# One wide matmul for a high weight and both parts of the input, in three of seven products of a fast matrix multiplication

## The chip, the cores and the metric

The kernel runs on one core of a Trainium2 chip. The metric is the device time of one execution in microseconds, the median of several runs. The engines are PE (TensorE, the matmuls), DVE (VectorE), ACT (ScalarE), POOL (GpSimd) and SP (SyncE, which here only issues DMAs).

## The reference

One layer of a decoder with two token mixers side by side; width 2048, 512 tokens, batch 1, all in float32. Cut to what matters:

```python
mod = silu(c) @ w_ada + b_ada
shift, scale, gate = split(mod, 3)
h = rmsnorm(x, attn_norm_g) * (1 + scale) + shift
proj = h @ w_in
q_lat, kv_lat, k_rope, z_mla, u, v, z_sgu, g_mla, g_sgu = split_cols(proj, IN_SPLITS)
...
y_mla = causal_mla_attention(q_nope, q_rope, k_nope, k_rope, v_mla) * silu(z_mla)
y_sgu = chunked_causal_sgu(u, v, sgu_norm_g, w_spatial, b_spatial) * silu(z_sgu)
merged = sigmoid(g_mla) * y_mla + sigmoid(g_sgu) * y_sgu
x = x + gate * (merged @ w_out)
return rmsnorm(x, final_norm_g)
```

`w_in` has 2048 rows; the five column blocks z_mla, g_mla, u, z_sgu and g_sgu are 2048 columns each. The attention has 16 heads with a rotary part of 64 columns whose key (`k_rope`) all heads share; its query and value come from the normalised latents `q_lat` (768) and `kv_lat` (512).

## The kernel before

**Arithmetic.** A float32 operand is split into a high part that PE takes at full speed and a low part, high plus low being the value. ACT copies the high part, DVE subtracts it from the value for the low part. A product is three matmuls into one PSUM bank: wH·xH, wH·xL and wL·xH (`mm3`, lines 135 to 137). Weights are split as they arrive, the input's parts `hh` and `hl` lie in 16 chunk tiles of 128 channels x 512 tokens each.

**Stages.** Up to 348 us: modulation, latents, v, and one plain tile of columns. From 348.2 to 1136.5 us: most column tiles (of 128 columns) of those five blocks, in 38 pairs (`PAIRS`, lines 34 to 36). Then attention, head by head, and the output projection.

**The slots.** A pair is a 2x2 block matrix product (two column tiles by two halves of the channels, against two halves of the channels by two halves of the tokens), done with seven products of sums of blocks instead of eight. A product is one slot: 8 chunks x 3 matmuls of 128x256 (lines 1267 to 1269). There are 266 slots, in an order written by hand, for a pair in the middle:

```python
turn_ = [(1, k), (6, k), (3, k - 1), (7, k), (4, k - 1), (5, k), (2, k)]
```

Products 1 to 4 of a pair write one bank ("y"), 6 and 7 another ("z"), 5 a third ("w"); `bank_for` gives the bank, always its first 256 columns. After its slot, a product is evacuated (`evacuate`): 1, 6, 2 and 4 are copied by ACT, 5, 3 and 7 are added or subtracted by DVE. When both halves of a column tile are there, `finish` puts the gate's operations (sigmoid on ACT, products on DVE) some slots later (`gate_op`). The right operand of product 4 and 5 is a token half of chunks 8 to 15 (`hh[8 + c][:, toks]` and the same of `hl`), that of product 7 the sum tiles `s4h` and `s4l`.

**What sets the order.** The program is written slot by slot; in each slot the events run in phases: evacuation of the slot ahead, FIRST, EVAC, GATE, SPLIT (the weights of the slot after next: ACT's copy, DVE's subtraction), BACK, then the slot's matmuls, then MISC and LOAD. BACK holds work for other stages (rotary tables, the spatial gating unit, the latents' norms), placed by a planner: `place` puts a job of so many us of DVE into the first slot whose charged time stays within 2.75 us; `spend` charges what is fixed. A tile is written again only when its readers are done, and so is a bank.

**Jobs named below.** `rope` computes the rotary tables on DVE in the first slots. Late in the stretch, `lat_store` writes the normalised latents to memory, `rope_load` fetches the tables (line 1122: eight DMAs on SP), `key_load` fetches the shared rotary key (line 1132: two DMAs), `key_turn` turns it on PE four slots later (line 1138), `key_rotary` rotates it on DVE in three jobs. The planner's slots for these are: tables computed up to slot 20, last latent norm 218, `key_load` 237, `key_turn` 241, key rotated by slot 245. The last pair's weights come in quarters (line 633). After the last slot, PE goes on with the rotary part of the query (`rproj`, 18 matmuls of 512 columns into bank 0), the query projection (`qproj`) of head 0 and its key projection (`kproj`).

Of the kernel before, what the change touches and what calls it, by code (L numbers as in the profile page):

```python
# [11 lines left out]
F32 = mybir.dt.float32  # L12
# [8 lines left out]
P = 128  # L21
# [94 lines left out]
def trunk_layer(ctx, tc, xT, xn, c, vecs, pos, wada, w1, w2, wv, wv3, wv4, wh, wh15, wq, wqr, wk, wvv, wo, wsT, bsp, gfin, out,  # L116
# [218 lines left out]

    hh, hl = [None] * KC, [None] * KC
    ssx = cosT
# [33 lines left out]
    for j in range(KC):  # L371
# [32 lines left out]
    def fix_to(n, between=None):  # L404
# [277 lines left out]
    for s in range(n_slots):  # L682
        def both(s=s):
            split_low(*split(s))
        on(s - 2, SPLIT, both)
    for k, pair in enumerate(PAIRS):
        at_ = slot_of[k]
        spend(at_[6] - 2, 1.22)
        for p, f in by_transfer(k).items():
            if not f:  # L690
                spend(at_[p] - 2, 1.22)
        for p in range(1, 8):
            spend(at_[p] - 2, 1.22)
# [58 lines left out]
    def evacuate(p, k, s):  # L752

        ps = bank_for(p, k)
        if p == 1:
# [7 lines left out]
        elif p == 5:  # L763
            t = res[k, "a"][:, left]
            tt(t, ps, t, ALU.add)
        elif p == 3:
            t = res[k, "b"][:, right]
            tt(t, t, ps, ALU.subtract)
        elif p == 4:
            ACT.copy(res[k, "a"][:, right], ps)  # L770
        if (p == 7 and slot_of[k][2] < slot_of[k][7]) or (p == 2 and slot_of[k][7] < slot_of[k][2]):
            def c12():
                t = res[k, "b"][:, left]
                tt(t, bank_for(7, k), t, ALU.subtract)
            if p == 7:
# [415 lines left out]

    def quarter(chunks, toks):
        return lambda c: (hh[chunks * 8 + c][:, toks], hl[chunks * 8 + c][:, toks])

    rights = {1: quarter(0, left), 2: sums_of("s2"), 3: quarter(0, right), 4: quarter(1, right), 5: quarter(1, left),
              6: sums_of("s1"), 7: sums_of("s4")}

# [58 lines left out]
    for s, (p, k) in enumerate(order):  # L1256
# [6 lines left out]
        for c in range(8):  # L1263
            xh, xl = rt_(c)
# [15 lines left out]

    place = {}
    for n, tag in (("krh", "hh10"), ("krl", "hl10"), ("m1", "hh11"), ("m2", "hl11"), ("r", "hh12"), ("qsa", "hl12"),
                   ("qsb", "hh13"), ("pt1", "hl13"), ("th0", "hh14"), ("tl0", "hl14"), ("th1", "hh15"), ("tl1", "hl15")):
        place[n] = (hp.p, tag)
# [377 lines left out]
```

## Time and profile before

| | |
|---|---|
| median of 3 runs | 1609.59 us (1609.11 to 1610.01) |
| profiled execution | 1609.98 us, its span 1608.3 us |
| PE busy | 1594.2 us, 99% of the span, 10760 matmuls |
| DVE busy | 1165.3 us, 72% |
| ACT busy | 755.5 us, 47% |
| POOL busy | 105.4 us, 7% |
| mean granted clock of PE | 0.999 |
| DMA | 329.64 MB, 205 GB/s over the span |

The span is the profiled execution between its first and last instruction. PE's busy time counts pipelined matmuls without their overlap, so a matmul's cost is read from the distance of starts, not from its duration.

### The profile page before, as it was taken

What the parts mean: (1) busy time and instruction counts of PE and PEld (TensorE: products, weight loads), DVE (VectorE), ACT (ScalarE), POOL (GpSimd) and SP (SyncE); (2) the same over time, 40 slices, a digit from 0 to 9 for tenths busy, and PEclk for the clock granted to TensorE, in tenths of its full rate; (3) what the DMA queues carried; (4) which work ended last, traced back from release to release, by engine and by line L of the source; (5) the groups of instructions that cost most, each with busy time, mean ns of one, the idle gap of its engine ahead of it and who ended that gap; (6) DMA issues with size and microseconds to landing.
All of it is one profiled execution on the core that took longest, in us unless ns stands there. A gap on an engine that the chain in (4) does not pass through costs nothing.

```text
span 1608.3 us, 26988 instructions
## 1 busy us (share of the span) xinstructions
PE 1594.2 (99%) x10760; PEld 1488.5 (93%) x10760; DVE 1165.3 (72%) x1719; ACT 755.5 (47%) x1259; POOL 105.4 (7%) x128
## 2 busy tenths in 40 slices
PE   9999999999999999999999999999999999999997
PEld 8888889999999999999999999999988889888886
DVE  8989679658777777777677777666777888763453
ACT  4443334355545454454465554554655554542322
POOL 0000000001111111111111111112000000000000
PEclk9999999999999999999999999999999999999999
DMA  9988489568899897898887998887422233336422
GB/s 379 354 296 317 171 280 324 170 193 202 219 253 252 226 252 214 233 258 212 231 253 203 250 268 207 238 193 181 162 87 88 82 105 89 90 109 227 136 87 105
DMA packets 122766, 329.64 MB, mean 205 GB/s; under 512 B 14072, under 2 KB 35600, under 8 KB 115856
## 3 DMA queue, kind: packets, MB, share of 16 engines
q1 hardware_dynamic: 104768, 269.72, 48.0%
q0 software_dynamic: 17872, 58.20, 20.8%
q8 instruction: 84, 1.38, 0.3%
q14 instruction: 42, 0.34, 0.1%
HBM read 303.95 MB, written 23.93 MB: 204 GB/s over the span
## 4 chain that ended last, share of the span: by engine, by line
PE 90%; DVE 4%; DMA 2%; ACT 1%; issue 1%; SPq 0%; DVEq 0%; ACTq 0%
PE ps L1267 15%; PE ps L1269 15%; PE ps L1268 15%; PE ps L136 14%; PE ps L137 14%; PE ps L135 14%; PE ps L1429 1%; DVE wada L126 1%; PE ps L1392 1%; PE ps L1393 1%; DVE t L123 1%; DMA wraw<-in_w 1%; DMA lat<-v_d 1%; DVE lat L123 1%; DMA rope_d<-half 0%
## 5 line engine op out<-in xcount | busy, mean ns | idle before, releaser
L106 DVE TENSOR_TENSOR w0l<-wraw,w0h 128x1024 fp32r<-128x1024 f32 (+3 forms) x74 | 78.8, 1066 | 58.8 <-ACT w0h L105 58.5
L105 ACT CAST w1h<-wraw 128x1024 fp32r<-128x1024 f32 (+3 forms) x74 | 63.9, 863 | 118.8 <-PE ps L137 57.7
L1267 PE MATMUL ps<-hh,w0h 128*128 128x256 f32 x416 | 118.5, 285 | 0.9 <-DVE lat L123 0.9
L105 ACT CAST w0h<-wraw 128x1024 fp32r<-128x1024 f32 (+3 forms) x74 | 68.9, 931 | 106.6 <-PE ps L137 66.5
L1269 PE MATMUL ps<-hh,w0l 128*128 128x256 f32 x416 | 117.7, 283 | 0.0
L1268 PE MATMUL ps<-hl,w0h 128*128 128x256 f32 x416 | 117.7, 283 | 0.0
L106 DVE TENSOR_TENSOR w1l<-wraw,w1h 128x1024 fp32r<-128x1024 f32 (+3 forms) x74 | 73.1, 988 | 59.6 <-ACT w1h L105 58.6
L1267 PE MATMUL ps<-hh,w2h 128*128 128x256 f32 x400 | 113.5, 284 | 0.0
L1267 PE MATMUL ps<-hh,w1h 128*128 128x256 f32 x400 | 113.4, 283 | 0.0
L1268 PE MATMUL ps<-hl,w1h 128*128 128x256 f32 x400 | 113.2, 283 | 0.0
L1269 PE MATMUL ps<-hh,w2l 128*128 128x256 f32 x400 | 113.2, 283 | 0.0
L1268 PE MATMUL ps<-hl,w2h 128*128 128x256 f32 x400 | 113.2, 283 | 0.0
L1269 PE MATMUL ps<-hh,w1l 128*128 128x256 f32 x400 | 113.2, 283 | 0.0
L126 DVE SCALAR_TENSOR_TENSOR wada<-wada,cact 128x2048 f32<-128x2048 f32 x47 | 107.1, 2280 | 0.0
L123 DVE TENSOR_TENSOR w2l<-raw,w2h 128x1024 fp32r<-128x1024 f32 x56 | 68.5, 1224 | 39.0 <-ACT w2h L649 38.9
L136 PE MATMUL ps<-w0l,hh 128*128 128x256 f32 (+3 forms) x288 | 92.7, 322 | 0.1
L135 PE MATMUL ps<-w0h,hh 128*128 128x256 f32 (+3 forms) x288 | 92.7, 322 | 0.0
L137 PE MATMUL ps<-w0h,hl 128*128 128x256 f32 (+3 forms) x288 | 92.4, 321 | 0.0
L135 PE MATMUL ps<-hh,w1h 128*128 128x512 f32 x226 | 89.7, 397 | 0.0
L136 PE MATMUL ps<-hl,w1h 128*128 128x512 f32 x226 | 88.3, 391 | 0.8 <-DVE hl L126 0.8
L137 PE MATMUL ps<-hh,w1l 128*128 128x512 f32 x226 | 88.1, 390 | 0.0
L629 POOL DMA_DIRECT2D wraw<-in_wh x67 | 59.2, 939 | 439.8 <-DVE w0l L123 211.7
(350 smaller groups left out, 5400.5 us busy)
## 6 DMA issues: line engine op xcount, KB each, us to landing
raw<-in_wh SPq DMA_DIRECT2D x105, 512.0 KB, 6.9
wada<-in_wada SPq DMA_DIRECT2D x47, 1024.0 KB, 7.4
wraw<-in_wh POOLq DMA_DIRECT2D x67, 512.0 KB, 6.9
wraw<-in_wh SPq DMA_DIRECT2D x45, 512.0 KB, 7.8
raw<-in_wh POOLq DMA_DIRECT2D x42, 512.0 KB, 7.8
wraw<-in_wo SPq DMA_DIRECT2D x32, 512.0 KB, 3.7
half<-in_w SPq DMA_DIRECT2D x35, 256.0 KB, 5.4
wraw<-in_w SPq DMA_DIRECT2D x16, 512.0 KB, 8.9
```

Source lines behind the costliest of these rows:

```text
L105: self.nc.scalar.copy(hi[:, :n], raw[:, :n])
L106: self.nc.vector.tensor_tensor(out=lo[:, :n], in0=raw[:, :n], in1=hi[:, :n].bitcast(F32), op=ALU.subtract)
L123: DVE.tensor_tensor(out=out, in0=in0, in1=in1, op=op)
L126: DVE.scalar_tensor_tensor(out=out, in0=in0, scalar=scalar, in1=in1, op0=op0, op1=op1, **kw)
L135: PE.matmul(ps, ah, bh, start=start, stop=False)
L136: PE.matmul(ps, ah, bl, start=False, stop=False)
L137: PE.matmul(ps, al, bh, start=False, stop=stop)
L629: q_.dma_start(t, wh[h, n, q // 10 - 1], **eng)
L1267: PE.matmul(ps, wH[:, sl], xh, start=st, stop=False, skip_group_check=True)
L1268: PE.matmul(ps, wH[:, sl], xl, start=False, stop=False, skip_group_check=True)
L1269: PE.matmul(ps, wL[:, sl], xh, start=False, stop=sp, skip_group_check=True)
L1392: PE.matmul(ps, q2[:, q], krh[:, :n], start=False, stop=False)
```

## The change

For products 4, 5 and 7 (`WIDE`), wH·xH and wH·xL become one matmul: the moving operand is `[xH | xL]` with 2 x 256 columns, and the bank's two halves take one product each; wL·xH is added into the first half as before. A slot of these has 16 matmuls instead of 24. The two halves are put together at the evacuation by one more DVE add of 128x256 per product. For this, `hh` and `hl` of a chunk become one tile of two parts (`parts_tiles`), and so do `s4h` and `s4l`. The evacuation of product 5 moves four slots later (one slot for the last pair). The planner charges each job 0.07 us less, and its limit becomes 2.7 us, 2.6 in a wide slot. The scratch tiles of attention are placed in the new tiles.

```diff
+WIDE = (4, 5, 7)
...
+    def parts_tiles(j):
+
+        hx[j] = nt(hp.p, [P, 2, S], F32R, f"h{j}")
+        return hx[j][:, 0], hx[j][:, 1]
...
+                sums["s4"] = nt(c1[0].p, [P, 8, 2, 256], F32R, "s4")
+                sums["s4h"], sums["s4l"] = sums["s4"][:, :, 0], sums["s4"][:, :, 1]
...
     def spend(s, us):
-        busy[s] = busy.get(s, 0.0) + us
+        busy[s] = busy.get(s, 0.0) + max(us - 0.07, 0.0)
 
     def place(s, us, f, *a):
 
-        while busy.get(s, 0.0) + us > 2.75:
+        while busy.get(s, 0.0) + us - 0.07 > (2.6 if 0 <= s < n_slots and order[s][0] in WIDE else 2.7):
             s += 1
...
+    def w_slot(k):
+
+        return slot_of[k][5] + (4 if k < n_pairs - 1 else 1)
...
-        for s in (at_[5] + 1, at_[3] + 1, at_[7] + 1 if at_[7] > at_[2] else at_[2] + 2):
-            spend(s, 0.42)
+        for p, s in ((5, w_slot(k)), (3, at_[3] + 1), (7, at_[7] + 1 if at_[7] > at_[2] else at_[2] + 2)):
+            spend(s, 0.84 if p in WIDE else 0.42)
+        spend(at_[4] + 1, 0.42)
...
+    def low_half(p, k):
+
+        return bank_for(p, k)[:, 256:]
...
         elif p == 5:
-            t = res[k, "a"][:, left]
-            tt(t, ps, t, ALU.add)
+            def c11():
+                t = res[k, "a"][:, left]
+                tt(t, ps, t, ALU.add)
+                tt(t, low_half(5, k), t, ALU.add)
+            on(w_slot(k), EVAC, c11)
...
         elif p == 4:
-            ACT.copy(res[k, "a"][:, right], ps)
+            t = res[k, "a"][:, right]
+            ACT.copy(t, ps)
+            tt(t, low_half(4, k), t, ALU.add)
...
-                tt(t, bank_for(7, k), t, ALU.subtract)
+                tt(t, bank_for(7, k)[:, :256], t, ALU.subtract)
+                tt(t, low_half(7, k), t, ALU.add)
...
+    rights = {1: quarter(left), 2: sums_of("s2"), 3: quarter(right), 4: lambda c: hx[c + 8][:, :, right],
+              5: lambda c: hx[c + 8][:, :, left], 6: sums_of("s1"), 7: lambda c: sums["s4"][:, c]}
...
-            PE.matmul(ps, wH[:, sl], xh, start=st, stop=False, skip_group_check=True)
-            PE.matmul(ps, wH[:, sl], xl, start=False, stop=False, skip_group_check=True)
-            PE.matmul(ps, wL[:, sl], xh, start=False, stop=sp, skip_group_check=True)
+            if p in WIDE:
+                x = rt_(c)
+                PE.matmul(ps.rearrange("p (e w) -> p e w", e=2), wH[:, sl], x, start=st, stop=False, skip_group_check=True)
+                xh = x[:, 0]
+            else:
+                xh, xl = rt_(c)
+                PE.matmul(ps[:, :256], wH[:, sl], xh, start=st, stop=False, skip_group_check=True)
+                PE.matmul(ps[:, :256], wH[:, sl], xl, start=False, stop=False, skip_group_check=True)
+            PE.matmul(ps[:, :256], wL[:, sl], xh, start=False, stop=sp, skip_group_check=True)
```

The planner's slots become: rotary tables computed up to slot 16, last latent norm 253, `key_load` 254, `key_turn` 258, key rotated by slot 265.

DVE in slot 6 (first the split made in slot 5, `w2l`, last that of slot 6; `lat<-ps` is an evacuation of product 7, `rx` and `half` are rotary work). Before:

```order
L123 TENSOR_TENSOR w2l_3324<-raw_301_3014,w2h_3323 128x1024
L123 TENSOR_TENSOR lat_350_3328<-lat_321_3131,lat_349_3327 128x512
L987 CAST rx_3135<-half_325_3137 128x128
L130 TENSOR_SCALAR rx_3135<-rx_3135,vec_88 128x128
L132 TENSOR_SCALAR rx_3135<-rx_3135 128x128
L123 TENSOR_TENSOR lat_335_3217<-ps_334_3192,lat_335_3217 128x256
L123 TENSOR_TENSOR w1l_3369<-raw_338_3248,w1h_3368 128x1024
```

Now:

```order
L124 TENSOR_TENSOR w2l_3277<-raw_268_2981,w2h_3276 128x1024
L124 TENSOR_TENSOR lat_317_3281<-lat_288_3102,lat_316_3280 128x512
L124 TENSOR_TENSOR rx_3106<-rx_3106 128x128
L133 TENSOR_SCALAR rx_3106<-rx_3106 128x128
L124 TENSOR_TENSOR rx_3106<-rx_3106 128x128
L131 TENSOR_SCALAR rx_3106<-rx_3106 128x128 x2
L133 TENSOR_SCALAR half_291_3107<-rx_3106 128x128
L124 TENSOR_TENSOR lat_302_3184<-ps_301_3159,lat_302_3184 128x256 x2
L124 TENSOR_TENSOR w1l_3326<-raw_305_3207,w1h_3325 128x1024
```

Product 7 has a second add, and six rotary operations stand here in the place of three.

SP's queue around the key's loads (`half<-kr_d`; `wraw` and `raw` are weights, `latn_d` is a store of the latents, `rope_d` the rotary tables). Before:

```order
L629 DMA wraw_1390_11618<-in_wh 128x1024
L748 DMA g_d_132<-lat_1351_11302 128x512
L629 DMA wraw_1394_11655<-in_wh 128x1024
L1132 DMA half_1399_11691<-kr_d 128x4x64 x2
L748 DMA g_d_132<-lat_1360_11375 128x512
L629 DMA raw_1403_11725<-in_wh 128x1024
L629 DMA raw_1408_11784<-in_wh 128x1024
L629 DMA raw_1416_11855<-in_wh 128x1024
```

Now:

```order
L638 DMA wraw_1407_11323<-in_wh 128x2x128 x4
L638 DMA raw_1412_11362<-in_wh 128x2x128 x4
L1091 DMA latn_d_130<-half_1390_11176 128x512
L1142 DMA cosT_11421<-rope_d 32x4x128 x4
L1142 DMA sinT_11422<-rope_d 32x4x128 x4
L1152 DMA half_1423_11453<-kr_d 128x4x64 x2
L634 DMA raw_1430_11512<-in_wh 128x1024
```

The key's loads stood between loads of weights; now they stand behind the last pair's quarter loads, the last store of the latents and the eight table loads.

DVE at the end of the slots (`w1l` and `w0l` with `wraw` are the splits for the rotary and the query projection, `hl` or `h` the low parts of the latents, `lat<-ps` the evacuations, `rx` the key's last rotary sum). Before:

```order
L106 TENSOR_TENSOR w1l_12606<-wraw_74_12522,w1h_12605 128x768
L126 SCALAR_TENSOR_TENSOR hl_1507_12610<-b_1485_12479,vec_88,hh_1506_12609 128x512
L126 SCALAR_TENSOR_TENSOR hl_1509_12614<-b_1486_12481,vec_88,hh_1508_12613 128x512
L126 SCALAR_TENSOR_TENSOR hl_1511_12618<-b_1487_12483,vec_88,hh_1510_12617 128x512
L123 TENSOR_TENSOR lat_1471_12369<-ps_1512_12621,lat_1471_12369 128x256
L126 SCALAR_TENSOR_TENSOR hl_1515_12652<-b_1488_12485,vec_88,hh_1514_12651 128x512
L126 SCALAR_TENSOR_TENSOR hl_1517_12656<-b_1489_12487,vec_88,hh_1516_12655 128x512
L106 TENSOR_TENSOR w0l_12684<-wraw_75_12555,w0h_12683 128x768
L123 TENSOR_TENSOR lat_1479_12435<-lat_1479_12435,lat_1513_12649 128x512
```

Now:

```order
L107 TENSOR_TENSOR w1l_11785<-wraw_74_11709,w1h_11784 128x768
L127 SCALAR_TENSOR_TENSOR h_1470_11788<-b_1450_11667,vec_88,h_1470_11788 128x512
L127 SCALAR_TENSOR_TENSOR h_1471_11791<-b_1451_11669,vec_88,h_1471_11791 128x512
L127 SCALAR_TENSOR_TENSOR h_1472_11794<-b_1452_11671,vec_88,h_1472_11794 128x512
L124 TENSOR_TENSOR lat_1434_11547<-ps_1473_11797,lat_1434_11547 128x256 x2
L124 TENSOR_TENSOR rx_11585<-lat_1459_11686,lat_1460_11687 128x512
L127 SCALAR_TENSOR_TENSOR h_1475_11821<-b_1453_11673,vec_88,h_1475_11821 128x512
L127 SCALAR_TENSOR_TENSOR h_1476_11824<-b_1454_11675,vec_88,h_1476_11824 128x512
L107 TENSOR_TENSOR w0l_11844<-wraw_75_11744,w0h_11843 128x768
L124 TENSOR_TENSOR lat_1434_11547<-ps_1433_11522,lat_1434_11547 128x256
```

The two products of the last pair that end here have second adds, the key's rotary sum has come in, and the last add, for product 4, stands behind the split for the query projection.

## Rows read from the trace of the kernel before

**Rows 1.** The page, part 1: busy us (share of the span) x instructions.
```profile
PE 1594.2 (99%) x10760; PEld 1488.5 (93%) x10760; DVE 1165.3 (72%) x1719; ACT 755.5 (47%) x1259; POOL 105.4 (7%) x128
```

**Rows 2.** Busy times by window: the stretch of the 266 slots.
```profile
core 0: us, PE busy (x) PEld busy (x) DVE busy (x) ACT busy (x) POOL busy (x), PEclk, DMA share, GB/s
...
348.20:1136.50 788.30, 785.63 (x6536) 783.63 (x6535) 577.17 (x751) 409.05 (x610) 101.84 (x117) 1.00 0.86 226
```

**Rows 3.** Timeline of PE in the slots (start us, us, instruction).
```profile
802.36 0.28 PE L1267 MATMUL ps<-s1h,w0h 128*128 128x256 f32 x1
...
805.24 0.28 PE L1267 MATMUL ps<-hh,w2h 128*128 128x256 f32 x1
```

**Rows 4.** Timeline of PE, late in attention.
```profile
1441.97 0.39 PE L135 MATMUL ps<-w0h,b 128*128 128x512 f32 x1
...
1445.37 0.39 PE L135 MATMUL ps<-w0h,b 128*128 128x512 f32 x1
```

**Rows 5.** Groups of DVE by form, 340 to 1140 us (busy, mean ns).
```profile
L123 DVE TENSOR_TENSOR lat<-lat,lat 128x512 f32<-128x512 f32 x91 | 62.3, 684 | 0.6
...
L123 DVE TENSOR_TENSOR lat<-ps,lat 128x256 f32<-128x256 f32 x76 | 31.8, 419 | 13.5 <-PE ps L1269 13.5
```

**Rows 6.** Timeline of DVE in the rotary work of before.
```profile
371.39 0.28 DVE L123 TENSOR_TENSOR rx<-rx 128x128 f32<-128x128 f32 x1
...
372.58 1.22 DVE L123 TENSOR_TENSOR w0l<-raw,w0h 128x1024 fp32r<-128x1024 f32 x1
373.71 0.22 DVE L132 TENSOR_SCALAR half<-rx 128x128 f32<-128x128 f32 x1
373.96 0.29 DVE L123 TENSOR_TENSOR half<-rx,half 128x128 f32<-128x128 f32 x1
```

**Rows 7.** Timeline of SP: rotary tables; last pair's loads.
```profile
993.04 2.21 SPq L1122 DMA_DIRECT2D cosT<-rope_d  x4
995.30 5.36 SPq L1122 DMA_DIRECT2D sinT<-rope_d  x4
1000.75 0.38 SPq L629 DMA_DIRECT2D raw<-in_wh  x1
...
1093.09 2.58 SPq L633 DMA_DIRECT2D wraw<-in_wh  x4
1095.78 2.62 SPq L633 DMA_DIRECT2D raw<-in_wh  x4
```

**Rows 8.** The rotary key's tensor in memory: its DMAs.
```profile
L1132 SPq DMA_DIRECT2D half<-kr_d x2: 695/748/800, 1052.0 to 1052.8; - x2
...
DMA to landing us min/median/max: 1.7/3.6/10.3
```

**Rows 9.** Timeline of PE: slot 218, the key's turn, the hand-over.
```profile
994.90 0.28 PE L1267 MATMUL ps<-s4h,w1h 128*128 128x256 f32 x1
...
1065.85 0.60 PE L1138 MATMUL ps<-ident,half 128*128 128x128 f32 x4
...
1136.48 0.40 PE L135 MATMUL ps<-hh,w1h 128*128 128x512 f32 x1
...
1144.66 0.39 PE L135 MATMUL ps<-hh,w1h 128*128 128x512 f32 x1
```

**Rows 10.** Timeline of DVE up to the hand-over.
```profile
1127.03 1.23 DVE L123 TENSOR_TENSOR w0l<-raw,w0h 128x1024 fp32r<-128x1024 f32 x1 [3.60 <-ACT w0h L649]
...
1139.13 0.95 DVE L106 TENSOR_TENSOR w0l<-wraw,w0h 128x768 fp32r<-128x768 f32 x1
```

**Rows 11.** Timeline of ACT at the hand-over.
```profile
1137.98 0.63 ACT L730 ACTIVATE lat<-lat 128x512 f32<-128x512 f32 x1 [0.93 <-DVE lat L123]
...
1143.16 0.62 ACT L105 CAST w1h<-wraw 128x512 fp32r<-128x512 f32 x1
```

**Rows 12.** Waits of DVE, 348 to 1165 us (total, times, longest).
```profile
DVE w2l L123 <- ACT w2h L649: 65.2, 63, 5.4
...
DVE w0l L123 <- ACT w0h L649: 59.5, 62, 3.6
```

More of the change, by code (lines that the diff above doesn't have):

```diff
@@ L334, in trunk_layer @@
         load_before(gv[0] + st + 1 if st < 31 else gv[0] + 31, ada_load, 2 * KC + j)
-    hh, hl = [None] * KC, [None] * KC
+    hh, hl, hx = [None] * KC, [None] * KC, [None] * KC
+    def parts_tiles(j):
+        hx[j] = nt(hp.p, [P, 2, S], F32R, f"h{j}")
+        return hx[j][:, 0], hx[j][:, 1]
     ssx = cosT
@@ L376, in trunk_layer @@
         wH, wL = get(g1[j], ahead=0)
-        hh[j] = nt(hp.p, [P, S], F32R, f"hh{j}")
-        hl[j] = nt(hp.p, [P, S], F32R, f"hl{j}")
+        hh[j], hl[j] = parts_tiles(j)
         ACT.activation(hh[j], xt[j], AF.Copy, scale=A)
@@ L421, in fix_to @@
         for j, t in zip(js, ts_):
-            hh[j] = nt(hp.p, [P, S], F32R, f"hh{j}")
+            hh[j], hl[j] = parts_tiles(j)
             ACT.activation(hh[j], t, AF.Identity, bias=shift[:, j:j + 1])
@@ L426, in fix_to @@
         for j, t in zip(js, ts_):
-            hl[j] = nt(hp.p, [P, S], F32R, f"hl{j}")
             stt(hl[j], t, shift[:, j:j + 1], hh[j].bitcast(F32), ALU.add, ALU.subtract)
@@ L693, in trunk_layer @@
             spend(at_[p] - 2, 1.22)
-        for s in (at_[5] + 1, at_[3] + 1, at_[7] + 1 if at_[7] > at_[2] else at_[2] + 2):
-            spend(s, 0.42)
-        for s, (ty, _) in ((max(at_[4], at_[5]), pair[0]), (max(at_[3], at_[7]), pair[1])):
+        for p, s in ((5, w_slot(k)), (3, at_[3] + 1), (7, at_[7] + 1 if at_[7] > at_[2] else at_[2] + 2)):
+            spend(s, 0.84 if p in WIDE else 0.42)
+        spend(at_[4] + 1, 0.42)
+        for s, (ty, _) in ((max(at_[4], w_slot(k) - 1), pair[0]), (max(at_[3], at_[7]), pair[1])):
             spend(s + 3, 1.38 if ty == "s" else 0.69)
@@ L715, in bank_for @@
     def bank_for(p, k):
-        return open_bank[k, "y" if p in (1, 2, 3, 4) else "z" if p in (6, 7) else "w"][:, :256]
+        return open_bank[k, "y" if p in (1, 2, 3, 4) else "z" if p in (6, 7) else "w"]
+    def low_half(p, k):
+        return bank_for(p, k)[:, 256:]
     gs, bs = {}, {}
@@ L752, in evacuate @@
     def evacuate(p, k, s):
-        ps = bank_for(p, k)
+        ps = bank_for(p, k)[:, :256]
         if p == 1:
@@ L781, in evacuate @@
         if p == max((4, 5), key=lambda q: slot_of[k][q]):
-            finish(k, "a", s + 1)
+            finish(k, "a", max(s, w_slot(k)) + 1)
     for j in range(8):
@@ L1182, in lat_split @@
     def lat_split(i):
-        lh[i] = nt(hp.p, [P, S], F32R, f"hh{i}")
-        ll[i] = nt(hp.p, [P, S], F32R, f"hl{i}")
+        lh[i], ll[i] = parts_tiles(i)
         g = vec[:, C_GQ + i:C_GQ + i + 1]
@@ L1190, in sums_of, with quarter @@
         return lambda c: (sums[name + "h"][:, c], sums[name + "l"][:, c])
[L1192 to L1196, printed above, removed]
+    def quarter(toks):
+        return lambda c: (hh[c][:, toks], hl[c][:, toks])
+    rights = {1: quarter(left), 2: sums_of("s2"), 3: quarter(right), 4: lambda c: hx[c + 8][:, :, right],
+              5: lambda c: hx[c + 8][:, :, left], 6: sums_of("s1"), 7: lambda c: sums["s4"][:, c]}
     def to_attention():
@@ L1279, in trunk_layer @@
         lat_split(i)
[L1281 to L1284, printed above, removed]
+    place, kept = {}, {}
+    for n, *where in (("krh", 10, 0), ("krl", 10, 1), ("m1", 11, 0), ("m2", 11, 1), ("r", 12, 0), ("pt1", 12, 1),
+                      ("qsa", 13, 0), ("qsb", 13, 1), ("th0", 14, 0), ("tl0", 14, 1), ("th1", 15, 0), ("tl1", 15, 1)):
+        place[n] = where
     for n, tag in zip(("vh0", "vl0", "qh", "ql", "kh", "kl", "vh1", "vl1", "pt3", "pt2", "th2"), range(11)):
-        place[n] = (latp.p, f"lat{tag}")
-    place["tl2"] = (latp.p, "rx")
+        place[n] = f"lat{tag}"
+    place["tl2"] = "rx"
     def at(name, dt, shape=(P, S)):
-        p, tag = place[name]
-        return nt(p, list(shape), dt, tag)
+        if isinstance(place[name], str):
+            return nt(latp.p, list(shape), dt, place[name])
+        i, e = place[name]
+        if i not in kept:
+            kept[i] = parts_tiles(i)
+        t = kept[i][e]
+        return t if dt is F32R else t.bitcast(F32)
     krh, krl = at("krh", F32R), at("krl", F32R)
```

3 lines of the change are left out of this document (removed).

## The prediction

> **What bounds the kernel now.** The page comes first: PE is busy for 1594.2 of 1608.3 us [rows 1], so an end that moves must move with PE's queue: fewer or shorter matmuls, or another wait in it. Next, the change touches only the 266 slots of the column pairs, so I read that stretch alone: from 348.2 to 1136.5, PE is busy for 785.63 of 788.30 us with a granted clock of 1.00, the 2.4 GHz level, which leaves 2.7 us of waiting in the whole stretch; DVE is busy for 577.17 us, 73% [rows 2]. So in this stretch the slots cost what the matmul stream costs. Then the stream itself: 24 matmuls of 256 columns start between 802.36 and 805.24 [rows 3], which is 120.0 ns each and 2.88 us for a slot. DVE has room on average, but it has to deliver three things on time: the low parts of the weights for the slot after next, the sum out of a bank before PE writes that bank again, and planned work for later stages. Where it runs late, PE waits.
>
> The sum is made on the profiled execution, 1609.98 us (1608.3 of span and 1.7 around it); the median of the runs shown, 1609.59, is 0.39 lower, so the result is carried over as a difference to the median.
>
> **Term 1, the matmuls.** In the slots of products 4, 5 and 7, eight pairs of 256-column matmuls become eight of 512 columns: 38 x 3 x 8 = 912 instructions fewer. The nearest rows for a 512-column matmul on this engine at the same clock are in attention's end: 15 start between 1441.97 and 1445.37 [rows 4], 226.7 ns each. Two of 256 columns take 240.0, so each merge saves 13.3 ns, a wide slot takes 8 x (226.7 + 120.0) = 2.77 us instead of 2.88, and 912 x 13.3 ns = **12.2 us** is the gross gain. It lies wholly on the path, since PE is the bound. The rows show that two starts cost more than one, by 13.3 ns for the same columns; I take that. The other end is 0: the operand of products 4 and 5 now consists of two pieces of 256 columns that don't lie side by side, and no row of before has a matmul with such an operand.
>
> The Trainium skill ("TensorE: Matmul & The Clock Gate", section "Back-to-back issue gap") gives for a lone matmul at the high clock a spacing of the columns over 2.4 plus 2.5 ns, which speaks against the change. By it, a merge would save only the 2.5 ns, an estimate of 2.3 us in all, and with the losses below the kernel would end at 1616.4. The rows above show 13.3 in the place of its 2.5.
>
> **Term 2, the adds on DVE.** Each wide product needs one more add of 256 columns out of the bank: 114 of them. Such an add takes 419 ns [rows 5], and as consecutive operations start some 0.08 us before the modelled end of the one ahead (a split of 1.22 us at 372.58, the next at 373.71 [rows 6]), I count 0.34, or 0.46 where it needs the result of the add just ahead of it. Together 39 to 52 us on DVE, which makes 616 to 629 of some 776 us, 80%. As a total this hides under PE and costs nothing. If that cover goes locally, PE waits; there are three places where it does.
>
> *The rotary work at the start (slots 6 to 8).* From one split to the next in slot 6, DVE now has the gate's product of 512 columns (684 ns [rows 5], so 0.60), six rotary operations, both adds of product 7 (0.80) and the split itself (1.13). Five rotary operations stand between 371.39 and 372.58 and one between 373.71 and 373.96 [rows 6]: 1.44. That makes 3.97 us against a slot of 2.77 to 2.88, 1.1 to 1.2 behind; in the order of before, the same slot holds three rotary operations and one add (0.60 + 0.72 + 0.34 + 1.13 = 2.79). The next slot has four rotary operations, 0.96, + 0.80 + 1.13 = 2.9 and stays behind. Queued behind this is the subtraction of product 3, which reads the bank that product 4 is to write next: late next are product 4's first matmul (slot 9), then low parts. PE waits a little over 1 us there; the rotary work goes on to slot 16 with such turns, so I take 3.0 us for the region. Bounds: 0.5 (splits are made two slots ahead, and that lead hides nearly all) and 4.0 (three full delays and a little).
>
> *The turn of the rotary key.* The planner places the late jobs differently: the rotary tables are now fetched after slot 253 (after 218 before) and the key after slot 254 (237 before), and the key is still turned on PE four slots later, at slot 258. On SP, the key's two loads now stand directly behind eight table loads, and these behind the eight loads of the last pair and a store that waits for DVE. Eight table loads took from 993.04 to 1000.75, 7.7 us; the last pair's eight loads 5.2 us [rows 7]. The key's loads need 10.3 us to land [rows 8]. In before nothing was behind them in time: issued at 1052.0, turned at 1065.85 [rows 8, 9]. Now 7.7 + 0.8 (the first of the two issues) + 10.3 = 18.8 us pass from the first table load to the key's landing, while six slots (253 to 258) last 16.9. If SP is 1.9 us ahead of PE, as it was at 993.04 against the slot's start at 994.90 [rows 7, 9], PE waits nothing or 0.3; if it is level, 1.9 plus a little; if the store delays it further by as much again, 4. The store and the sixteen loads leave it no lead: I take **2.3**, bounds 0.3 and 4.2. All of PE's queue stands behind the turn.
>
> *The hand-over to attention.* The query projection uses the bank of the last product 4, so its first matmul waits for that product's new low-half add, which is queued on DVE behind the splits for attention. Before, the last split for the query projection, 1139.13 plus 0.95 [rows 10], was done 3.6 us after the last slot's end at 1136.48 [rows 9], inside the 4.1 us of the rotary projection (18 matmuls at 226.7 ns). Now two second adds (0.92), the key's last rotary sum (0.60) and the final add (0.36) come ahead: 3.6 + 1.9 = 5.5 us, a wait of 1.4. The key's two rotary products also move to the last slots, and up to 1.5 us of them reaches the end, though the idle 3.6 us before 1127.03 [rows 10] can take some: 1.4 to 2.9, I take 2.2. Behind it, ACT's sigmoid (1137.98) waits for the same add, and the weights for the key projection come last in ACT's queue, at 1143.16 plus 0.62 [rows 11]: 5.4 us of work after the sigmoid's start. That ends 6.3 + 5.4 = 11.7 us after the slots' end, while PE gets there after 8.2 (1144.66 [rows 9]) + 2.2 = 10.4: 1.0 more, after rounding down for overlap. Together **3.2**, bounds 1.4 and 4.4.
>
> *The rest.* The evacuation of product 5 comes four slots later; its bank is not needed before the next pair's product 5, seven slots on: nothing. Placing scratch tiles elsewhere adds no instruction: nothing. The waits of before (2.7 us) may shift; 0.6, bounds 0 and 1.2.
>
> **Sum.** -12.2 + 3.0 + 2.3 + 3.2 + 0.6 = -3.1: 1609.98 becomes 1606.9, and the median **1606.5**. With all lower bounds -10.0 (1599.6), with all upper ones +1.6 (1611.2).
>
> **Rivals.**
> (1) *DVE's lead covers the three places*: splits run two slots ahead, and the idle in rows 10 shows room; against it stands the count of slot 6. Losses at their lower bounds: 1599.6.
> (2) *Slower: the second adds become a regular delay.* The place is every turn of a pair: an add that waits for its product stands ahead of a split, and one add in three is not covered. Price: 38 x 0.34 = 12.9 us on top, 1619.4. It decides where DVE's idle ahead of a split is under 0.34 us. Against it: in the slot stretch DVE waits for ACT's high parts some 60 times for each weight buffer, 65.2 us in 63 times and 59.5 in 62 [rows 12], 1 us each. For it: that idle is not spread evenly, and the planner fills slots to 2.6 us.
> (3) *Slower: the wide matmul saves little.* If an operand in two pieces is read as two, the 76 slots of products 4 and 5 save nothing, 76 x 8 x 13.3 ns = 8.1 us less, 1614.6; if no merge saves anything, 1618.7. It decides with the step of a wide matmul: 240 ns instead of 226.7. Nothing in the trace speaks for it but that such an operand is not in it; against it, product 7's operand is contiguous and the contiguous rows are plain. (The page of the Trainium skill named above lies between the two with its 2.5 ns.)
>
> **Chances.** The forecast 0.75, (1) 0.12, (2) 0.08, (3) 0.05. A measurement of this kernel can tell about 0.2%, 3.2 us, from no change, so faster is below 1606.4 and slower above 1612.8. The forecast lies on the faster bound and its losses are as likely above as below: 0.33 faster and 0.42 the same. With (1), faster has 0.45; (2) and (3) give slower 0.13. The range takes in (1) and the upper bounds of the forecast, 1599.5 to 1611.2, and leaves out (2) and (3).
>
> **What will show it.** Steps of PE of 226.7 and 120 ns by turns in a wide slot, 2.77 us for it; a wide slot of 2.88 for product 4 but not for 7 would be rival (3). The slot stretch shorter by some 6 to 7 us, with new waits of PE: on DVE's `lat` near slot 9, on the key's load before the turn, and on `lat` at the first matmul of the query projection. Waits of 0.3 us in every pair would be rival (2); none of the three, rival (1). The prediction is wrong if the wide matmul's step isn't near 227 ns, or if PE's waits in the stretch and at the hand-over don't sum to 8 to 14 us with those of before.

## The result and the profile after

The changed kernel takes 1612.19 us (median of 22 runs, 1610.39 to 1614.00) against 1609.62 for the kernel before, a ratio of 1.0014 with the interval [1.0008, 1.0021]: 2.6 us slower, where 3.1 faster was forecast, and 1.0 above the stated range. By the bound of 0.2% it counts as no change. The profiled execution has a span of 1609.9 us, 1.6 above that of before. Cut at three places of PE's timeline, this is where the 1.6 comes from (slots: from the first slot's first matmul to the rotary projection's first; hand-over: from there to the first matmul of the value projection):

| | before | changed | |
|---|---|---|---|
| first slot starts | 348.23 | 347.89 | -0.3 |
| slots | 788.25 | 786.29 | -2.0 |
| hand-over | 10.91 | 14.98 | +4.1 |
| the rest, to the end | 460.9 | 460.7 | -0.2 |

So 12.2 us of expected gain less 5.9 of expected losses became 2.0 in the slots, and the hand-over took twice that. Engine totals of the changed kernel (the page, part 1, as [rows 1]) and the busy times of the slots (window, as [rows 2]):

```profile
PE 1590.5 (99%) x9848; PEld 1440.5 (89%) x9848; DVE 1210.5 (75%) x1833; ACT 755.2 (47%) x1259; POOL 104.6 (6%) x128
```

```profile
347.90:1136.00 788.10, 782.25 (x5631) 736.42 (x5630) 620.99 (x862) 409.32 (x610) 102.24 (x117) 1.00 0.86 226
```

912 matmuls are gone, DVE has 44 us more in the slots, 79% of the window, as reckoned. PE's timeline in two wide slots, product 7 (`ps<-s`) and product 4 (`ps<-h`), up to the next slot's extra work:

```profile
805.97 0.40 PE L1288 MATMUL ps<-s,w1h 128*128 128x512 f32 x1
806.21 0.28 PE L1294 MATMUL ps<-s,w1l 128*128 128x256 f32 x1
806.32 0.40 PE L1288 MATMUL ps<-s,w1h 128*128 128x512 f32 x1
...
808.80 0.40 PE L1288 MATMUL ps<-h,w0h 128*128 128x512 f32 x1
809.04 0.28 PE L1294 MATMUL ps<-h,w0l 128*128 128x256 f32 x1
...
811.62 0.29 PE L850 MATMUL ps<-whl,lat 128*128 128x256 f32 x1
```

Product 7 takes 2.83 us (805.97 to 808.80) and product 4 takes 2.82: not the 2.77 of the sum, nor 2.88. The 512-column matmul is followed after 0.24 us, the 256-column one after 0.11 to 0.12; over all 912 pairs the medians are 236 and 118 ns. PE's waits, 340 to 1180 us (total, times, longest):

```profile
PE ps L1288 <- DVE lat L124: 2.5, 3, 1.4
PE ps L136 <- DVE lat L124: 1.9, 1, 1.9
PE ps L1294 <- DVE w1l L124: 1.3, 2, 0.8
PE ps L1288 <- ACT lat L774: 0.8, 1, 0.8
PE ps L1294 <- DVE w2l L124: 0.6, 2, 0.3
PE ps L1292 <- ACT w1h L654: 0.4, 1, 0.4
PE ps L1294 <- DVE w0l L124: 0.3, 1, 0.3
```

Without the second line, which is the hand-over's, these sum to 5.9 us, where before had 2.7. The hand-over on PE's timeline; the first column is the start, the bracket the wait ahead:

```profile
1138.26 0.39 PE L138 MATMUL ps<-h,w1l 128*128 128x512 f32 x1
1140.59 0.50 PE L136 MATMUL ps<-h,w0h 128*128 128x512 f32 x1 [1.95 <-DVE lat L124]
...
1141.73 0.63 PE L137 MATMUL ps<-h,w0h 128*128 128x512 f32 x1
1142.16 0.63 PE L138 MATMUL ps<-h,w0l 128*128 128x512 f32 x1
...
1145.04 0.40 PE L136 MATMUL ps<-h,w0h 128*128 128x512 f32 x1
...
1146.42 0.39 PE L136 MATMUL ps<-h,w1h 128*128 128x512 f32 x1
```

PE waits 1.95 us at the query projection's first matmul, and then steps of 0.43 us follow (1141.73 to 1142.16), nearly double. The projection's 18 matmuls take 5.83 us up to the key projection (1140.59 to 1146.42), where 18 of 226.7 ns would take 4.08. The windows tell why (the column PEclk is the granted clock, 1.00 for 2.4 GHz):

```profile
core 0: us, PE busy (x) PEld busy (x) DVE busy (x) ACT busy (x) POOL busy (x), PEclk, DMA share, GB/s
1116.00:1120.00 4.00, 2.65 (x23) 2.48 (x21) 2.84 (x4) 2.59 (x4) 0.00 (x0) 1.00 1.02 335
...
1141.00:1145.00 4.00, 4.00 (x12) 3.14 (x11) 2.77 (x5) 3.94 (x8) 0.00 (x0) 0.57 0.67 230
1145.00:1149.00 4.00, 4.00 (x19) 3.22 (x19) 2.20 (x3) 2.46 (x4) 0.00 (x0) 1.00 0.95 324
```

Between 1141 and 1145 the mean is 0.57: PE runs at its lower level, 1.2 GHz, for most of it. DVE's queue at this place:

```profile
1137.33 0.68 DVE L124 TENSOR_TENSOR rx<-lat,lat 128x512 f32<-128x512 f32 x1
1137.93 1.41 DVE L127 SCALAR_TENSOR_TENSOR h<-b,vec,h 128x512 fp32r<-128x512 f32 x2
1139.25 0.95 DVE L107 TENSOR_TENSOR w0l<-wraw,w0h 128x768 fp32r<-128x768 f32 x1
1140.12 0.42 DVE L124 TENSOR_TENSOR lat<-ps,lat 128x256 f32<-128x256 f32 x1
```

The last line is the second add of product 4. It ends just before PE starts at 1140.59, behind the split at 1139.25 and the key's rotary sum at 1137.33, as the prediction had it. The key's turn, on the other hand, didn't wait. The tile's DMAs, as [rows 8], and the turn on PE:

```profile
L1152 SPq DMA_DIRECT2D half<-kr_d x2: 382/420/457, 1103.2 to 1103.9; - x2
...
DMA to landing us min/median/max: 1.7/3.7/5.1
```

```profile
1112.24 0.60 PE L1158 MATMUL ps<-ident,half 128*128 128x128 f32 x4
```

Issued at 1103.9 with at most 5.1 us to landing, the key is there by 1109, 3 us ahead of its turn.

### The profile page after: what moved, and what is told of

Same layout as the page of the kernel before. It is cut to its first block, busy times and chain, and to the rows that moved or that the text cites. A ratio compares the mean times of both kernels' runs of the same rounds, so it can differ in the third digit from the quotient of the medians.

```text
span 1609.9 us, 25341 instructions
## 1 busy us (share of the span) xinstructions
PE 1590.5 (99%) x9848; PEld 1440.5 (89%) x9848; DVE 1210.5 (75%) x1833; ACT 755.2 (47%) x1259; POOL 104.6 (6%) x128
## 4 chain that ended last, share of the span: by engine, by line
PE 87%; DVE 6%; DMA 3%; ACT 3%; issue 1%; SPq 0%; DVEq 0%; ACTq 0%
PE ps L137 14%; PE ps L138 14%; PE ps L136 14%; PE ps L1294 14%; PE ps L1288 11%; PE ps L1293 8%; PE ps L1292 8%; PE ps L1459 1%; DMA lat<-v_d 1%; DVE lat L124 1%; DVE wada L127 1%; DVE w1l L124 1%; PE ps L1422 1%; PE ps L1423 1%; DVE t L124 1%
## 5 line engine op out<-in xcount | busy, mean ns | idle before, releaser
L124 DVE TENSOR_TENSOR lat<-ps,lat 128x256 f32<-128x256 f32 (+1 forms) x238 | 112.1, 475 | 32.6 <-ACT lat L788 21.5
L1294 PE MATMUL ps<-h,w0l 128*128 128x256 f32 x416 | 117.4, 282 | 0.0
L1294 PE MATMUL ps<-h,w2l 128*128 128x256 f32 x400 | 113.0, 282 | 0.3 <-DVE w2l L124 0.3
L1294 PE MATMUL ps<-h,w1l 128*128 128x256 f32 x400 | 112.9, 282 | 0.0
L137 PE MATMUL ps<-w0l,h 128*128 128x256 f32 (+3 forms) x288 | 92.8, 322 | 0.0
L136 PE MATMUL ps<-w0h,h 128*128 128x256 f32 (+3 forms) x288 | 92.8, 322 | 0.0
L138 PE MATMUL ps<-w0h,h 128*128 128x256 f32 (+3 forms) x288 | 92.5, 321 | 0.0
L136 PE MATMUL ps<-h,w1h 128*128 128x512 f32 x226 | 89.9, 398 | 0.0
L137 PE MATMUL ps<-h,w1h 128*128 128x512 f32 x226 | 88.4, 391 | 0.7 <-DVE h L127 0.7
L138 PE MATMUL ps<-h,w1l 128*128 128x512 f32 x226 | 88.3, 391 | 0.0
L136 PE MATMUL ps<-h,w0h 128*128 128x512 f32 x198 | 78.8, 398 | 1.9 <-DVE lat L124 1.9
L1288 PE MATMUL ps<-h,w0h 128*128 128x512 f32 x216 | 78.1, 402 | 2.0 <-DVE lat L124 2.0
L1294 PEld LDWEIGHTS ps<-h,w0l 128*128 128x128 f32 x416 | 79.1, 190 | 0.2 <-issue 0.2
L137 PE MATMUL ps<-h,w0h 128*128 128x512 f32 x198 | 77.9, 394 | 0.0
```

What stands on the lines that cost most here:

```text
L124: DVE.tensor_tensor(out=out, in0=in0, in1=in1, op=op)
L136: PE.matmul(ps, ah, bh, start=start, stop=False)
L137: PE.matmul(ps, ah, bl, start=False, stop=False)
L138: PE.matmul(ps, al, bh, start=False, stop=stop)
L1288: PE.matmul(ps.rearrange("p (e w) -> p e w", e=2), wH[:, sl], x, start=st, stop=False, skip_group_check=True)
L1294: PE.matmul(ps[:, :256], wL[:, sl], xh, start=False, stop=sp, skip_group_check=True)
```

## The experiments

Four theories were tried: (A) the merge is worth half because 512- and 256-column matmuls alternate; (B) the wide matmul itself costs more; (C) a wait of 2 us at the hand-over costs as much again through the clock; and for the slots' losses, the second adds or the planner's new places. Slots and hand-over are cut as above, in the profiled execution; the medians come from runs beside the kernel before (1609.67 to 1609.83). Executions that have the same slots but for their last pair differ in the slots by 0.3 to 1.0 us (before and d1, changed and t1, b1 and b2), so differences of that size between two rows say nothing.

| kernel | wide slot | slots | hand-over | median us | ratio |
|---|---|---|---|---|---|
| before | | 788.25 | 10.91 | 1609.62 | |
| changed | 2.83 | 786.29 | 14.98 | 1612.19 | 1.0014 [1.0008, 1.0021] |
| g1_grouped | 2.79 | 783.41 | 15.10 | 1607.52 | 0.9988 [0.9978, 0.9997] |
| u1_unmerged | 2.88 | 791.77 | 14.79 | 1617.17 | 1.0048 [1.0033, 1.0063] |
| t1_tail | 2.83 | 785.99 | 11.13 | 1607.38 | 0.9988 [0.9979, 0.9997] |
| d1_delay | | 787.75 | 14.69 | 1613.52 | 1.0021 [1.0012, 1.0031] |
| g2_group_tail | 2.79 | 782.94 | 11.12 | 1604.42 | 0.9968 [0.9956, 0.9981] |
| n1_no_adds | 2.83 | 786.95 | 11.63 | 1606.99 | 0.9981 [0.9971, 0.9990] |
| pb_places | | 791.90 | 11.51 | 1615.80 | 1.0038 [1.0024, 1.0052] |
| a0_oldplan | 2.83 | 782.97 | 13.61 | 1606.16 | 0.9978 [0.9969, 0.9987] |
| b1_best | 2.79 | 779.41 | 12.61 | 1602.04 | 0.9951 [0.9939, 0.9964] |
| b2_first | 2.79 | 780.44 | 12.64 | 1603.25 | 0.9959 [0.9947, 0.9972] |
| b3_oldplan | 2.79 | 779.65 | 10.91 | 1600.51 | 0.9944 [0.9931, 0.9956] |

**What the merge is worth.** In g1_grouped only the order within a wide slot changes:

```diff
             if p in WIDE:
-                x = rt_(c)
-                PE.matmul(ps.rearrange("p (e w) -> p e w", e=2), wH[:, sl], x, start=st, stop=False, skip_group_check=True)
-                xh = x[:, 0]
+                PE.matmul(ps.rearrange("p (e w) -> p e w", e=2), wH[:, sl], rt_(c), start=st, stop=False, skip_group_check=True)
+                continue
...
+        if p in WIDE:
+            for c in range(8):
+                sl = slice(c * P, (c + 1) * P)
+                PE.matmul(ps[:, :256], wL[:, sl], rt_(c)[:, 0], start=False, stop=c == 7, skip_group_check=True)
```

> The changed kernel, with the 16 matmuls of a wide slot in another order: first the eight of 512 columns, then the eight of 256. Theory A (the loss is in the alternation: a 256-column matmul behind a 512-column one starts 236 ns after it instead of 226.7, and the pair takes 353.5 ns instead of 346.7): the wide steps become 227 ns, the narrow ones 120, a wide slot 2.78 us instead of 2.83, and the kernel gains about 114 x 0.05 = 5.7 us, so about 1606.5; the low parts of the weights are needed later in a wide slot, which may take up to 1 us of PE's waits on DVE away. Theory B (a matmul that writes both halves of a bank costs some 9 ns more by itself): the wide steps stay at 236 ns, the time at 1612.2.

The slot of a product 4 on its timeline (grouped by like operations, count at the end):

```profile
807.11 2.00 PE L1287 MATMUL ps<-h,w0h 128*128 128x512 f32 x8
808.95 1.12 PE L1296 MATMUL ps<-h,w0l 128*128 128x256 f32 x8
809.90 0.28 PE L850 MATMUL ps<-whl,lat 128*128 128x256 f32 x1
```

Eight wide matmuls from 807.11 to 808.95, 230 ns each, and eight narrow ones in 0.95 us, 119 each. Over the kernel a wide matmul behind a wide one in the slots starts after 231 ns (median of 798), a narrow one behind a narrow one after 120; a slot takes 2.79 us, the slots are 2.9 us shorter and the median is 4.7 lower (the profiled execution lies 1.5 above the median). So theory A has most of the loss (0.04 of the 0.05 to 0.06 us of a slot), and what theory B could still claim is 4 ns of a wide matmul. A narrow matmul behind a wide one is not late as such: behind the last wide one of a slot it starts here after 227 ns (median of 114). The 236 ns show only where the widths alternate. What in PE makes them, and what the 4 ns are, isn't shown by any view.

u1_unmerged takes each wide matmul apart again and leaves the rest:

```diff
-                PE.matmul(ps.rearrange("p (e w) -> p e w", e=2), wH[:, sl], x, start=st, stop=False, skip_group_check=True)
                 xh = x[:, 0]
+                PE.matmul(ps[:, :256], wH[:, sl], xh, start=st, stop=False, skip_group_check=True)
+                PE.matmul(ps[:, 256:], wH[:, sl], x[:, 1], start=False, stop=False, skip_group_check=True)
```

> The changed kernel with each wide matmul taken apart into two of 256 columns, the low part's product still into the bank's second half; all adds and the planner's order stay. So the merge's own worth is read. By the steps seen in the changed kernel (353.5 ns for 512 + 256 against 360): 912 x 6.5 ns = 5.9 us slower than the changed kernel, 1618.1. By the step the prediction used (346.7): 12.2 us slower, 1624.4.

It is 5.0 us slower than the changed kernel by the medians, and 5.5 in the slots (791.77 less 786.29). Its narrow matmuls step by 120 ns (median) also where they write the bank's second half. So the merge as written gives 5 to 5.5 us, not 12.2, and everything else that came with it costs 3.5 in the slots (791.77 less 788.25).

**The hand-over.** t1_tail keeps the last pair narrow and moves one split:

```diff
-    on(n_slots - 1, MISC, lambda: ws.split_to(gq[0]))
+    on(n_slots - 1, SPLIT, lambda: ws.split_to(gq[0]))
...
-            if p in WIDE:
+            if p in WIDE and k < n_pairs - 1:
```

> The changed kernel, but the last pair's three products stay narrow (no second add for them) and the split of the query projection's weights is made one phase earlier, ahead of DVE's last latents. The wait of 1.95 us at the first matmul of the query projection should go. Theory C (the wait also drops PE's clock, and the half-clock matmuls behind it cost as much again): the granted clock stays at 1.00 there and the kernel gains about 4 us, 1608.2. Rival (only the wait counts): about 2 us, 1610.2.

PE at the query projection's start, and at the key projection's:

```profile
1136.67 0.39 PE L138 MATMUL ps<-h,w1l 128*128 128x512 f32 x1
1136.89 0.39 PE L136 MATMUL ps<-h,w0h 128*128 128x512 f32 x1
...
1140.97 0.39 PE L136 MATMUL ps<-h,w1h 128*128 128x512 f32 x1
```

No wait: 0.22 us from the last rotary matmul to the next. The 18 matmuls of the query projection take 4.08 us (1136.89 to 1140.97), 227 ns each, as at the full clock. The hand-over falls by 3.85 us to 11.13, twice the wait that was removed, and the median by 4.8. Theory C is borne out; its counter-test puts the wait into the kernel before:

```diff
+        hi, lo = ws.hl[gq[0]]
+        for _ in range(3):
+            tt(lo[:, :768], ws.last_raw[:, :768], hi[:, :768].bitcast(F32), ALU.subtract)
```

> The kernel before, with the subtraction for the query projection's weights made four times instead of once on DVE: 3 x 0.87 = 2.6 us later, less some 0.5 of spare, so PE waits about 2.1 us at the query projection. Theory C: the granted clock falls to its lower level behind that wait, and the time rises by about 4 us, 1613.6. Rival: it rises by 2.1 us, 1611.7, and the clock stays.

```profile
1142.07 0.75 PE L138 MATMUL ps<-hh,w0l 128*128 128x512 f32 x1 [1.91 <-DVE w0l L124]
1142.61 0.63 PE L136 MATMUL ps<-hh,w0h 128*128 128x512 f32 x1
1143.04 0.63 PE L137 MATMUL ps<-hl,w0h 128*128 128x512 f32 x1
...
1145.58 0.40 PE L137 MATMUL ps<-hl,w0h 128*128 128x512 f32 x1
```

The windows of the same stretch:

```profile
1142.00:1146.00 4.00, 3.94 (x10) 3.16 (x11) 3.74 (x7) 0.69 (x2) 0.00 (x0) 0.57 0.64 202
1146.00:1150.00 4.00, 4.00 (x19) 3.30 (x19) 1.52 (x2) 1.53 (x2) 0.00 (x0) 1.00 1.01 341
```

A wait of 1.91 us, then again steps of 0.43 us (1142.61 to 1143.04) and a mean clock of 0.57. The hand-over grows by 3.8 us and the median by 3.8, for 1.9 of waiting. g2_group_tail joins both edits:

> Both edits that helped, together: wide slots with the eight wide matmuls first, and the hand-over with the last pair narrow and the query projection's split earlier. If the two losses (5 us in the slots by the alternation, 5 us at the hand-over by the wait and the clock) are separate, the gains add: about 1612.2 - 4.7 - 4.8 = 1602.7. If one hides behind the other, about 1607.

1604.42: most of both gains, 7.8 of 9.5 us. In the parts both are there in full, 3.35 in the slots and 3.86 at the hand-over, so the two losses are separate.

**The slots' losses.** n1_no_adds leaves the second adds out, and with them the product of the high weights and the low input for products 4, 5 and 7:

```diff
-                tt(t, low_half(5, k), t, ALU.add)
...
-            tt(t, low_half(4, k), t, ALU.add)
...
-                tt(t, low_half(7, k), t, ALU.add)
```

> The changed kernel without the 114 second adds on DVE; the product of the high weights and the low input of products 4, 5 and 7 is left out of the result by this. Everything else stays. If the adds cause PE's new waits (1.6 us in the rotary work, 1.1 near 1027, 0.5 near 1120, and the hand-over), all of them go: about 3 us in the slots and 4 to 5 at the hand-over, 1604 to 1605. If the planner's later places cause them (tables, key and last latents pushed to the end), the hand-over and the waits near 1027 and 1120 stay, and it gains under 2.5 us, about 1610.

Its median falls by 5.2, and neither forecast came whole: the hand-over is 3.35 shorter, while the slots of its profiled execution aren't shorter at all (786.95 against 786.29), and PE's waits in them sum to 6.3 us against 5.9. That is one execution, 2.2 us above its median, and its record gives a granted clock of 0.95 from end to end although its steps are the 236, 118 and 120 ns of the changed kernel, which no view explains. So pb_places puts the question the other way round: the kernel before, with nothing of the change but its planner.

```diff
-        busy[s] = busy.get(s, 0.0) + us
+        busy[s] = busy.get(s, 0.0) + max(us - 0.07, 0.0)
...
-        while busy.get(s, 0.0) + us > 2.75:
+        while busy.get(s, 0.0) + us - 0.07 > (2.6 if 0 <= s < n_slots and order[s][0] in (4, 5, 7) else 2.7):
...
+            spend(s, 0.84 if p in (4, 5, 7) else 0.42)
```

> The kernel before with the changed planner alone: its charges, its limits and the adds charged as if they were there, so that every planned job stands in the slot that it has in the changed kernel; no wide matmul, no second add, product 5 evacuated as before. If the places cause the changed kernel's 3.6 us of losses in the slots, the slot stretch takes about 791 us instead of 788.2, and the time is about 1612.5. If the second adds cause them, it stays at 788 and 1609.7.

The slots take 791.90 us, 3.65 more than before, without a single added operation. They are also level with those of u1_unmerged (791.77), which has as many matmuls of the same widths and the same places, and runs the 114 adds. DVE and ACT there:

```profile
398.80 0.43 DVE L123 TENSOR_TENSOR wsr<-wsr,tri 128x256 f32<-128x256 f32 x1 [1.69 <-DMA wsr<-in_wsT]
...
402.33 1.28 ACT L1013 ACT_TABLE_LOAD   x1
...
404.49 1.05 ACT L649 CAST w2h<-raw 128x1024 fp32r<-128x1024 f32 x1
```

A job of the spatial unit now comes before its weights have landed: DVE stands 1.69 us. ACT, which needs its result, then has a scaling, a table load and three sines for the rotary tables ahead of the cast of `w2h`, and PE waits 0.76 us for that split (406.85). The changed kernel has the same row of jobs on ACT there: DVE stands only 0.29 us for the transfer, the cast starts at 405.11 and PE waits 0.33 us (407.47). In the kernel before the sines' table load comes at 411.18, ten us behind this cast. The median of 1615.80 is even 2.9 above the profiled execution (1612.92); what the other executions lose is not seen. The opposite edit, a0_oldplan, gives the changed kernel the planner of before, with the adds running uncharged:

```diff
-        busy[s] = busy.get(s, 0.0) + max(us - 0.07, 0.0)
+        busy[s] = busy.get(s, 0.0) + us
...
-        while busy.get(s, 0.0) + us - 0.07 > (2.6 if 0 <= s < n_slots and order[s][0] in WIDE else 2.7):
+        while busy.get(s, 0.0) + us > 2.75:
...
-            spend(s, 0.84 if p in WIDE else 0.42)
-        spend(at_[4] + 1, 0.42)
+            spend(s, 0.42)
```

> The changed kernel with the planner of before (its charges and its limit of 2.75 us; the second adds run but are not charged), so every planned job stands where it stood before. If the new places cause the 3.6 us of losses in the slots, these take 782.7 to 783 us instead of 786.3, the key's rotary work leaves the hand-over, and the time is about 1608; with the adds as the cause of them it stays at 786 and 1612.

The slots take 782.97, 3.3 less, and the median is 1606.16, 6.0 less. So the places cost the slots 3.3 us and the 114 adds nothing that stands out of the scatter: 788.25 less 114 merged slots' 5.6 (2.88 less 2.83, before rounding) would be 782.65. A second place where the new places collide can be read from the changed kernel's own trace, ACT near 1022:

```profile
1021.13 1.28 ACT L836 ACTIVATE lat<-lat,rv 128x128 f32<-128x128 f32 x4 [1.46 <-DMA lat<-v_d]
1022.43 1.28 ACT L1080 ACT_TABLE_LOAD   x1
1023.72 0.69 ACT L1080 ACTIVATE rx<-ps,eps 128x512 f32<-128x512 f32 x1
1024.43 1.28 ACT L744 ACT_TABLE_LOAD   x1
1025.72 0.63 ACT L744 ACTIVATE lat<-lat 128x512 f32<-128x512 f32 x1
1026.26 1.03 ACT L654 CAST w1h<-raw 128x1024 fp32r<-128x1024 f32 x1
```

```profile
1027.32 1.23 DVE L124 TENSOR_TENSOR w1l<-raw,w1h 128x1024 fp32r<-128x1024 f32 x1 [4.55 <-ACT w1h L654]
```

Scaling for the spatial unit, a square root with a table load and a sigmoid with another stand ahead of the cast of `w1h`; DVE waits 4.55 us for it, and PE 0.4 and 0.8 us behind. The planner charges DVE's time alone and doesn't see ACT. In a0_oldplan two short waits stay at the hand-over:

```profile
1135.96 0.50 PE L136 MATMUL ps<-h,w0h 128*128 128x512 f32 x1 [0.80 <-DVE lat L124]
...
1141.38 0.50 PE L136 MATMUL ps<-h,w1h 128*128 128x512 f32 x1 [1.03 <-ACT w1h L106]
```

They are 0.80 and 1.03 us, and no drop of the clock is seen there. The hand-over thus needs the adds: it is 0.6 us longer than before with the new places alone (pb_places), 0.7 without the adds (n1_no_adds), 2.7 with the adds in the old places (a0_oldplan) and 4.1 with both.

**A faster version.** b1_best joins g2's edits with three more:

> As g2_group_tail, and three more edits: in every slot the eight matmuls with the low weights come last, the second add of product 4 stands behind the split on DVE instead of ahead of it, and in the last turn product 2 goes between products 3 and 4 of the pair ahead. The first should take away PE's waits on low parts of weights (2.2 us in the changed kernel), the last the wait of 1.35 us near 1120. About 1602.7 - 3 = 1599.5; if DVE's lateness only moves on to the next wait, 1602.7.

```diff
-            turn_ = [(1, k), (6, k), (2, k), (3, k - 1), (4, k - 1), (3, k), (7, k), (5, k), (4, k)]
+            turn_ = [(1, k), (6, k), (3, k - 1), (2, k), (4, k - 1), (3, k), (7, k), (5, k), (4, k)]
...
-                tt(t, low_half(4, k), t, ALU.add)
+                on(s, SPLIT, tt, t, low_half(4, k), t, ALU.add)
...
+        if wide or LAST:
+            for c in range(8):
+                sl, x = slice(c * P, (c + 1) * P), rt_(c)
+                PE.matmul(ps[:, :256], wL[:, sl], x[:, 0] if p in WIDE else x[0], start=False, stop=c == 7, skip_group_check=True)
```

1602.04, a little short of the hoped 1599.5: the slots are 3.5 us shorter than g2's, as hoped, but the hand-over is 1.5 longer, with a wait of 0.72 us for the rotary projection's split. b2_first, one split earlier, gained nothing (1603.25):

```diff
-    on(n_slots - 2, SPLIT, lambda: ws.split_to(gr[0]))
+    on(n_slots - 2, FIRST, lambda: ws.split_to(gr[0]))
```

> As b1_best, with the split of the rotary projection's weights one phase group earlier, ahead of the gate's products on DVE: its wait of 0.72 us at the first slot after the products should go, 1601.3; if DVE's queue only moves on, 1602.0.

b3_oldplan is b1_best with the planner of before, the edit of a0_oldplan:

> As b1_best, with the planner of before. Its remaining waits of PE on DVE (2.8 us) should fall by about 2 if the places cause them: 1600. If uncharged adds overfill slots in the rotary work, new waits there, 1602 to 1604.

1600.51, 0.9944 [0.9931, 0.9956]: the fastest, 9.2 us under the kernel before in the runs beside it. What is left of PE's waits:

```profile
PE ps L1292 <- DVE lat L125: 1.5, 2, 0.8
PE ps L1295 <- DVE lat L125: 1.2, 1, 1.2
PE ps L1292 <- ACT lat L774: 0.8, 1, 0.8
```

The time is the one expected, but not by the way that was expected: the waits on DVE are still 2.7 us, and the slots are no shorter than b1's (779.65 against 779.41). The gain is at the hand-over, which is that of before again, 10.91, 1.7 less than in b1. So in b1's order the planner's places cost the slots nothing that is seen; the 3.3 us hold for the changed kernel's.

## Why the prediction was wrong

- **Term 1, the matmuls: the failing step.** "Each merge saves 13.3 ns" took the step of a wide matmul from rows in which another wide one follows ([rows 4]). In this kernel the two widths alternate, and the pair takes 354 ns instead of 346.7: the wide step is 236 ns, which the prediction itself named as a sign of being wrong. The 12.2 us measured 5 to 5.6. Rival (3) had the size in its neighbourhood but not the reason: product 7's contiguous operand is as slow as those in two pieces. The Trainium skill's rule ("TensorE: Matmul & The Clock Gate", "Back-to-back issue gap") would have had 2.3 us by estimate; the runs lie above it, 6 ns a merge in alternation and 9 when grouped.
- **The hand-over: the mechanism right, the size short.** 3.2 was forecast, 4.1 measured. The wait (2.2 forecast, 1.95 seen) was where it was said to be, and the wait of 1.0 at the key projection did not come. In its place PE ran at 1.2 GHz behind the wait, which the sum did not have at all: the query projection took 1.75 us longer than at the full clock. The remaining 0.4 lies in the step into the wait and the rotary projection's first steps.
- **The rotary work: the waits came, by half.** From 348 to 435 us they are 2.6 us, beside 0.8 that was there before, against 1.0 in the kernel before: 1.6 more, where 3.0 was taken. The count of slot 6 had two causes, 0.72 us for three more rotary operations (the places) and 0.46 for the second add. The first wait came where the prediction put it, at product 4 in slot 9 (0.63 us), and before, pb_places and n1_no_adds have none there. But without the adds others take its place: n1_no_adds waits 3.4 us in this region too, and a0_oldplan, with the same adds, loses 0.3 in all its slots. So in the sum the places count, not the added work. The region alone decides less: from execution to execution its waits differ by 1 us (3.4 in all here, 2.3 in t1_tail, whose program is the same there).
- **The key's turn: wrong.** 2.3 us were taken, nothing was seen. The step that failed was the landing time, 10.3 us from [rows 8]: here 5.1 (the eight table loads held SP for 6.8 us, near the 7.7 taken). One row's longest is no price for another moment of the queues.
- **The rest** held 0.6 and was 1.6: 1.1 near 1027, from ACT, which the prediction didn't look at, and 0.5 at 1120.
- Summed: -5.6 + 3.6 + 4.1 = +2.1 in the place of -3.1 (the profiled execution moved by +1.6, the medians by +2.6). Of the 5.2 us between the two, term 1 brought 6.6 and the hand-over 0.9, and losses set too high gave 2.3 back. The waits sum to 7.8 us (5.9 and 1.95), just under the 8 to 14 that the prediction named. That the adds as a total would hide under PE, and that rival (2) was unlikely, was right.

## What to carry to other kernels

Price an instruction by rows in which the same neighbours stand before and after it: a merge that leaves wide and narrow matmuls by turns was worth half of what rows among their like gave. When a change also moves planned work, time the moved places alone; in this kernel's slots they cost over half of what the merge gave. And a wait of PE should be priced with the clock behind it.

## What was not expected of the hardware

- Where 512- and 256-column matmuls alternate, the narrow one starts 236 ns behind the wide one (2.4 GHz) and the wide one 118 behind the narrow one. Among its like a narrow one steps by 120, a wide one by 227 in attention and 231 in the slots of g1_grouped, where the narrow one behind a slot's last wide one comes after 227 too.
- Waits of PE of 1.95 and 1.91 us were each followed by some 3.4 us at 1.2 GHz (PEclk 0.57 over 4 us), which doubled their cost; waits of 0.80, 1.03 and 1.4 us (the last in the changed kernel's window 1116 to 1120 above, PEclk 1.00) were not. All the waits that were followed by it stand at the hand-over, so whether their length alone decides isn't shown. The Trainium skill ("TensorE: Matmul & The Clock Gate", "HAM oscillation — how this bites in real kernels") describes matmuls at half speed behind waits for data of some 3 to 5 us; the two traces show the same behind shorter ones.
